# Small steps of each norm in a fixed sequence, weights split on one engine, and the values' product ahead of the gates'

## The chip, the core and the metric

The kernel runs on one core of a Trainium2 chip, as one program. TensorE (PE) multiplies matrices, VectorE (DVE), ScalarE (ACT) and GpSimd (POOL) do the rest, and SyncE (SP) issues the transfers. Each engine works through its own instructions in the order in which they were written; semaphores make it wait for others. The metric is the time of an execution on the device in microseconds (us), less is better.

## The reference

The input is 256 tokens of width 1024 in float32. A first block of two layers (window, stick-breaking and block attention with gates, then a gated feed-forward part with a short convolution) ends in an rms norm. The change touches only what the second block shares with it, the split of weights, and the second block's own layers:

```python
for l in range(2):
    hcat = x @ w_in[l]   # r_q r_k r_v r_g (256 each), c_q c_kv k_r, m_q m_k m_v m_o (256 each), m_i m_f
    ret   = retention(rope(r_q), rope(r_k), r_v)                       # 4 heads of 64
    ret_out   = silu(r_g) * (head_norm(ret) * ret_gn_w[l])
    att_out   = mla_attention(...)                                     # 8 heads of 64, from c_q, c_kv, k_r
    hcell     = num / max(abs(den), exp(-m_t))                         # mlstm(m_q, m_k, m_v, m_i, m_f)
    mlstm_out = head_norm(sigmoid(m_o) * hcell) * mlstm_gn_w[l]
    x = layer_norm(ALPHA * x + concat(ret_out, att_out, mlstm_out) @ w_out[l])
    f = swiglu(x) if l == 0 else moe_swiglu(x)                         # 8 experts of 3584, each token in 2
    x = layer_norm(ALPHA * x + f)

def head_norm(x, w, n):          # per token and head
    mu, var = mean(x), mean((x - mu)**2)
    return (x - mu) * rsqrt(var + 1e-5) * w
```

## The kernel before

Each float32 product is made of three (`mm3`): an operand is split into a high part that PE takes exactly and a low part with the rest, and high·high, high·low and low·high are added up. So every weight is split on the way. SP loads it in pieces of 1 MB into buffers (`raw`, and parts of `b24a`, `b24b`, `const` and `mixed` that are lent later on); ACT copies 128x1024 of it into `whi` (`Weights.high`); then `raw - whi` is written to `wlo` (`Weights.low`). This subtraction is called the split here. There are about a thousand of them, and `low` chooses the engine: POOL, if a layer norm is under way (`g.calm`) or if POOL would be done earlier than DVE by more than the constant `POOL`, and DVE otherwise. `g.quiet` keeps splits off POOL. Splits are made ahead of use into five pairs of buffers (`PIECES`).

The order on each engine is fixed when the program is built. A planner in Python writes the matmuls in sequence, and keeps a model of time for every engine (`Meter`). Between matmuls, `Ctx.tick` looks through lists of tasks (`first`, `urgent`, `tasks`, `heads`) and writes what the model holds to be ready. A task is a Python generator: at each `yield` it gives way to others, or waits for a condition. Because a split belongs to `urgent`, it can come between any two steps of a norm that are parted by a `yield`. All instructions are recorded under one line, L163, in the wrapper `Counted`.

A layer of the second block runs as follows. `second_mixer` multiplies x by parts of `w_in` in the order of `plan_second` and queues the heads (retention `ret_pair`, mLSTM `mlstm_pair`, latent attention `mla`), whose small matmuls come between those of the projections. `ret_norm` and `mlstm_norm` call `head_norm` for each half t of the tokens (128 each), transpose the result on PE (matmuls with `const`) and split it into the operand of the product with `w_out`. That product adds up eight blocks of 128 rows in the order `MIX_ORDER`: blocks 0 and 1 are the retention's, 2 to 5 the attention's, 6 and 7 the mLSTM's. `out_ln` runs this product and `layer_norm` on its result: addition to x with statistics in two halves of 512 columns, the small steps of `rstd` (a scale on POOL, then a power −0.5 on POOL), two steps on x with mean and weight, two with the factor and bias. The result is transposed (matmuls of `const` and `X`), split into `hTh` and `hTl` and meets the next weights. Layer 0 has a dense feed-forward part (`dense_ffn`), layer 1 a routing followed by eight experts. The tail of a mixer is the end of this product, where PE waits for the head norms.

Of the kernel before, what the change touches and what calls it, by code (L numbers as in the profile page):

```python
# [17 lines left out]
P = 128  # L18
# [177 lines left out]
class Weights:  # L196
# [67 lines left out]
    def low(self, i, hi, lo, raw, piece, buf, last):  # L264
        g = self.g
        m = g.m
        n = lo.free_size()
        pool = lambda: max(m.t["gpsimd"], m.floor) + 2.3 * n
        if g.calm and pool() > g.calm[0]:
            yield lambda: not g.calm or pool() <= g.calm[0]  # L270
        dve = max(m.t["vector"], m.floor) + 1.04 * n
        eng = g.nc.gpsimd if g.calm or pool() + POOL < dve and not g.quiet else g.nc.vector
        eng.tensor_tensor(lo, raw, hi, op=ALU.subtract)
        self.done[i] = (hi, lo, piece)
        self.low_done += 1
# [47 lines left out]
class Ctx:  # L323
# [5 lines left out]
    def __init__(self, ctx, tc, a):  # L329
# [9 lines left out]
        self.calm = []  # L339
# [208 lines left out]
POOL, SLACK, EARLY, EARLY_MOE = 1000.0, 0.0, 4000.0, 1500.0  # L548
# [725 lines left out]
def last_norm(g, fT, done, X):  # L1274
# [16 lines left out]
    def post(t, o):  # L1291
# [6 lines left out]
        rstd(g, ss[:, 3:4], ss[:, 2:3], D, 1e-6)  # L1298
# [18 lines left out]
def head_norm(g, r, mult, out):  # L1317
# [10 lines left out]
    yield  # L1328
    rs = sm[:, 12:16]
    rstd(g, rs, mv[:, :, 1], 1.0, 1e-5)  # L1330
    yield
    for h in range(4):
        nc.vector.tensor_scalar(r[:, h, :], r[:, h, :], mv[:, h, 0:1], rs[:, h:h + 1], op0=ALU.subtract, op1=ALU.mult)
    g.give(sm)
    nc.vector.tensor_tensor(out, r.rearrange("p h d -> p (h d)"), mult, op=ALU.mult)


def plan_second(g, l):
# [9 lines left out]
    plan_t(g, w, 1952, 512)  # L1348
    plan_t(g, w, 512, 512)
# [10 lines left out]
MIX_ORDER = [2, 3, 4, 5, 6, 7, 0, 1]  # L1360
# [4 lines left out]
def second_mixer(g, x, l, hT, ready):  # L1365
# [104 lines left out]
    def latents(t, o):  # L1470
# [15 lines left out]
        rstd(g, r, ss, 256, 1e-5)  # L1486
# [147 lines left out]
    def ret_norm(t):  # L1634
        yield got("ret", 2)
        yield got(f"sg{t}")
        yield lambda: g.free["t10"] and g.free["small"]
        r = g.take("t10")
        yield from head_norm(g, heads_out["ret"][1][:, t], sg[:, t, :], r)
# [38 lines left out]
    def mlstm_norm(t):  # L1678
        yield got("mlstm", 2)
        yield got(f"so{t}")  # L1680
        yield lambda: g.free["t10"] and len(g.free["small"]) >= 2
        r = g.take("t10")
        hh = heads_out["mlstm"][1]
# [5 lines left out]
        sv = so[:, t, :].rearrange("p (h d) -> p h d", h=4)  # L1689
# [57 lines left out]
    def mvo(t, o):  # L1747
        nc.vector.tensor_copy(vX[:, t, :, 0:64], o[:, 0:256].rearrange("p (h d) -> p h d", h=4))
        g.act(so[:, t, :], o[:, 256:512], AF.Tanh, scale=0.5)
        g.give(o)  # L1750
        done.mark("mv")
        yield
        nc.gpsimd.tensor_scalar(so[:, t, :], so[:, t, :], 1.0, None, op0=ALU.add)
    for t in range(2):
        g.do(count(f"so{t}", mvo(t, o[t])))
# [4 lines left out]
    def rvg(t, o):  # L1760
        nc.scalar.activation(rv[:, t, :], o[:, 0:256], AF.Copy)
        g.act(sg[:, t, :], o[:, 256:512], AF.Tanh, scale=0.5)
        done.mark("rv")
        yield got("along")
        nc.vector.scalar_tensor_tensor(sg[:, t, :], sg[:, t, :], 1.0, o[:, 256:512], op0=ALU.add, op1=ALU.mult)
        g.give(o)
        yield
        nc.gpsimd.tensor_tensor(sg[:, t, :], sg[:, t, :], rw, op=ALU.mult)
    for t in range(2):
        g.do(count(f"sg{t}", rvg(t, o[t])))  # L1770
# [6 lines left out]
    def over():  # L1777

        yield got("mla", 4)
        g.quiet += 1  # L1780
# [3 lines left out]
        g.quiet -= 1  # L1784
# [33 lines left out]
def layer_norm(g, x, o, wb, bb, free=None, half=None):  # L1818
# [6 lines left out]
    g.calm.append(max(g.m.floor, g.m.t["vector"]) + 2700)  # L1825
# [769 lines left out]
```

## Time and profile before

| | |
|---|---|
| median of 3 runs | 2377.19 us (2376.48 to 2380.56) |
| the profiled execution | 2376.09 us, span 2374.4 us |
| mean granted clock of PE | 0.991 |
| PE, DVE, ACT, POOL busy | 97%, 78%, 63%, 17% of the span |
| POOL, splits of `raw` | 35, 93.5 us in all, 2672 ns each |
| DVE, splits of `raw` | 597, 748.4 us in all, 1280 ns each |

Of 40 slices of the span, the first 23 or so are the first block and the mixers with the dense part; from about 1400 us on the experts run, in which the transfers' share of the 16 engines is 0.9 and above, and from 1640 us on POOL does nothing. The granted clock is 1.00 nearly everywhere; it falls in a few short stretches, around and behind waits of PE. What a wait of PE costs is its own length and what such a stretch adds.

### The profile page before, as it was taken

The page shows a single profiled execution, that of the slowest core. Times are in us where ns is not written, and L with a number is a line of the kernel's source. Part 1 is how long each engine was busy: PE and PEld are TensorE (multiplying, and loading weights), DVE is VectorE, ACT ScalarE, POOL GpSimd, SP SyncE. Part 2 cuts the span into 40 slices and gives each one's busy share as a digit, 9 for nine tenths or more (in the row PEclk, how much of TensorE's full clock was granted, in tenths as well). Part 3 has the DMA queues.
Part 4 walks back from the last instruction along what each step waited for, and adds up shares of the span by engine and source line. Part 5 has one row for each costly group of instructions (what it writes and reads, how often), then busy time and mean ns, then how long its engine had stood idle before and what let it go on. Part 6 is the DMA issues. An engine that isn't in the chain of part 4 may idle for free. (4 is left out here: it accounts for less than half of the span.)

```text
span 2374.4 us, 36554 instructions
## 1 busy us (share of the span) xinstructions
PE 2298.7 (97%) x13593; PEld 1958.9 (83%) x13593; DVE 1851.4 (78%) x2618; ACT 1490.6 (63%) x2144; POOL 407.3 (17%) x417
## 2 busy tenths in 40 slices
PE   8999999999999999989999889989999999999997
PEld 7799999988999988779978668767888767888764
DVE  6666897665589856775568778899888899898898
ACT  4664566465646645634436457777777787777785
POOL 5202343224043312220022320220000000000000
PEclk9999999999999999999999999999999999999999
DMA  7345555543555564355654569999999899999894
GB/s 246 124 127 193 167 187 186 191 136 115 177 178 162 194 215 156 107 169 187 221 156 135 200 246 333 348 378 375 366 344 364 332 389 397 371 337 360 321 373 171
DMA packets 267951, 577.77 MB, mean 243 GB/s; under 512 B 12818, under 2 KB 138354, under 8 KB 267508
## 3 DMA queue, kind: packets, MB, share of 16 engines
q1 hardware_dynamic: 267764, 575.35, 68.4%
q8 instruction: 108, 1.77, 0.3%
q14 instruction: 79, 0.65, 0.1%
HBM read 574.27 MB, written 1.05 MB: 242 GB/s over the span
## 5 line engine op out<-in xcount | busy, mean ns | idle before, releaser
L163 DVE TENSOR_TENSOR wlo<-raw,whi 128x1024 fp32r<-128x1024 f32 (+1 forms) x597 | 748.4, 1280 | 195.1 <-ACT whi L163 191.9
L163 ACT ACTIVATE whi<-raw 128x1024 fp32r<-128x1024 f32 (+1 forms) x632 | 643.0, 1042 | 169.3 <-PE bank L163 140.8
L163 PE MATMUL bank<-hTh,whi 128*128 128x256 f32 x1064 | 306.1, 288 | 0.2 <-ACT const L163 0.2
L163 PE MATMUL bank<-hTl,whi 128*128 128x256 f32 x1064 | 301.4, 283 | 0.0
L163 PE MATMUL bank<-hTh,wlo 128*128 128x256 f32 x1064 | 301.3, 283 | 0.0
L163 PE MATMUL bank<-whi,b8c 128*128 128x512 f32 x752 | 247.7, 398 | 0.0
L163 PE MATMUL bank<-whi,b8a 128*128 128x512 f32 x672 | 234.2, 403 | 0.0
L163 DVE TENSOR_TENSOR wlo<-b24b,whi 128x1024 fp32r<-128x1024 f32 x168 | 201.5, 1244 | 13.5 <-ACT whi L163 12.8
L163 PEld LDWEIGHTS bank<-hTh,whi 128*128 128x128 f32 x1064 | 201.8, 190 | 3.6 <-issue 1.5
L163 PEld LDWEIGHTS bank<-hTh,wlo 128*128 128x128 f32 x1064 | 201.6, 190 | 0.1
L163 PEld LDWEIGHTS bank<-hTl,whi 128*128 128x128 f32 x1064 | 201.7, 190 | 0.0
L163 PE MATMUL bank<-whi,hTl 128*128 128x512 f32 (+2 forms) x540 | 196.5, 386 | 0.0
L163 PE MATMUL bank<-wlo,b8a 128*128 128x512 f32 x448 | 182.0, 406 | 8.9 <-DVE wlo L163 5.4
L163 ACT ACTIVATE whi<-b24b 128x1024 fp32r<-128x1024 f32 x172 | 174.0, 1056 | 13.9 <-PE bank L163 12.7
L163 POOL TENSOR_TENSOR wlo<-raw,whi 128x1024 fp32r<-128x1024 f32 (+1 forms) x35 | 93.5, 2672 | 515.0 <-ACT whi L163 492.3
L163 PE MATMUL bank<-wlo,b8c 128*128 128x512 f32 x432 | 173.5, 402 | 6.1 <-DVE wlo L163 6.1
L163 PEld LDWEIGHTS bank<-whi,b8c 128*128 128x128 f32 x752 | 140.9, 188 | 31.7 <-issue 1.0
L163 PEld LDWEIGHTS bank<-whi,b8a 128*128 128x128 f32 x672 | 126.3, 189 | 30.3 <-issue 2.4
L163 DVE TENSOR_TENSOR wlo<-b24a,whi 128x1024 fp32r<-128x1024 f32 x121 | 143.2, 1224 | 5.8 <-ACT whi L163 5.6
L163 PE MATMUL bank<-whi,hTh 128*128 128x512 f32 (+2 forms) x348 | 138.3, 397 | 0.0
L163 POOL TENSOR_SCALAR small<-small 128x1 f32<-128x1 f32 (+2 forms) x15 | 4.4, 293 | 779.5 <-DVE small L163 778.6
L163 PE MATMUL bank<-b8a,whi 128*128 128x256 f32 x480 | 136.3, 284 | 0.0
(317 smaller groups left out, 5229.4 us busy)
## 6 DMA issues: line engine op xcount, KB each, us to landing
raw<-in_w_in_dram SPq DMA_DIRECT2D x68, 1024.0 KB
raw<-in_moe_w_up_dram SPq DMA_DIRECT2D x47, 1024.0 KB
raw<-in_w_up_dram SPq DMA_DIRECT2D x44, 1024.0 KB
raw<-in_moe_w_gate_dram SPq DMA_DIRECT2D x43, 1024.0 KB
raw<-in_moe_w_down_dram SPq DMA_DIRECT2D x34, 1024.0 KB
b24b<-in_moe_w_up_dram SPq DMA_DIRECT2D x33, 1024.0 KB
b24b<-in_moe_w_down_dram SPq DMA_DIRECT2D x32, 1024.0 KB
b24a<-in_moe_w_down_dram SPq DMA_DIRECT2D x27, 1024.0 KB
```

Of the source, the lines that this page charges most:

```text
L163: r = f(*a, **kw)
```

## The change

Splits are made by DVE alone and not while `g.quiet` is set, which `layer_norm` now sets from its small steps to its last step on x. The small steps are written without a `yield` between them, the first of them on DVE. In `out_ln` the norm of the second half of the tokens waits until that of the first is written. In `head_norm` the scaling by mean and factor moves from DVE to ACT (Identity with scale and bias), for which a shift −mean·rs is made; the multiplication by the gate or weight is done by the callers. `mlstm_norm` divides by the denominators with one broadcast multiplication per half. In `plan_second` and `second_mixer` the product for the values (r_v, m_v) comes ahead of that for the gates (r_g, m_o). `MIX_ORDER` puts the retention's blocks ahead of the mLSTM's.

```diff
 class Weights: def low(self, i, hi, lo, raw, piece, buf, last):
-        pool = lambda: max(m.t["gpsimd"], m.floor) + 2.3 * n
-        if g.calm and pool() > g.calm[0]:
-            yield lambda: not g.calm or pool() <= g.calm[0]
-        dve = max(m.t["vector"], m.floor) + 1.04 * n
-        eng = g.nc.gpsimd if g.calm or pool() + POOL < dve and not g.quiet else g.nc.vector
-        eng.tensor_tensor(lo, raw, hi, op=ALU.subtract)
+        if g.quiet:
+            yield lambda: not g.quiet
+        g.nc.vector.tensor_tensor(lo, raw, hi, op=ALU.subtract)
...
-def rstd(g, out, var, n, eps):
+def rstd(g, out, var, n, eps, by="vector"):
-    g.nc.gpsimd.tensor_scalar(out, var, 1.0 / n, eps, op0=ALU.mult, op1=ALU.add)
+    getattr(g.nc, by).tensor_scalar(out, var, 1.0 / n, eps, op0=ALU.mult, op1=ALU.add)
     g.nc.gpsimd.tensor_tensor(out, out, g.half[:, :m], op=ALU.pow)
...
 def head_norm:
-    yield
-    rs = sm[:, 12:16]
+    rs, shift = sm[:, 12:16], sm[:, 16:20]
     rstd(g, rs, mv[:, :, 1], 1.0, 1e-5)
+    nc.vector.tensor_scalar(shift, mv[:, :, 0], -1.0, None, op0=ALU.mult)
+    nc.gpsimd.tensor_tensor(shift, shift, rs, op=ALU.mult)
     yield
     for h in range(4):
-        nc.vector.tensor_scalar(r[:, h, :], r[:, h, :], mv[:, h, 0:1], rs[:, h:h + 1], op0=ALU.subtract, op1=ALU.mult)
+        nc.scalar.activation(out[:, h, :], r[:, h, :], AF.Identity, scale=rs[:, h:h + 1], bias=shift[:, h:h + 1])
     g.give(sm)
-    nc.vector.tensor_tensor(out, r.rearrange("p h d -> p (h d)"), mult, op=ALU.mult)
+    yield
...
 def plan_second:
-    plan_t(g, w, 1952, 512)
-    plan_t(g, w, 512, 512)
+    for c in (0, 256):
+        for k0 in (0, 4):
+            k = slice(k0 * P, (k0 + 4) * P)
+            g.w.add([w[k, 512 + c:768 + c], w[k, 1952 + c:2208 + c]], 4, 512, [(0, 2, 0, 512), (2, 4, 0, 512)])
...
-MIX_ORDER = [2, 3, 4, 5, 6, 7, 0, 1]
+MIX_ORDER = [2, 3, 4, 5, 0, 1, 6, 7]
...
 def ret_norm:
-        yield from head_norm(g, heads_out["ret"][1][:, t], sg[:, t, :], r)
+        yield from head_norm(g, heads_out["ret"][1][:, t], r.rearrange("p (h d) -> p h d", h=4))
+        nc.gpsimd.tensor_tensor(r, r, rw, op=ALU.mult)
+        yield got(f"sg{t}")
+        nc.vector.tensor_tensor(r, r, sg[:, t, :], op=ALU.mult)
...
 def mlstm_norm:
-        for h in range(4):
-            nc.vector.scalar_tensor_tensor(hh[:, t, h, :], hh[:, t, h, :], den[:, h:h + 1], sv[:, h, :],
-                                           op0=ALU.mult, op1=ALU.mult)
+        nc.vector.tensor_tensor(hh, hh, den[:, :, None].to_broadcast([P, 4, 64]), op=ALU.mult)
-        yield from head_norm(g, hh[:, t], mw, r)
+        yield got(f"so{t}")
+        nc.vector.scalar_tensor_tensor(hh, so[:, t, :].rearrange("p (h d) -> p h d", h=4), 1.0, hh, op0=ALU.add,
+                                       op1=ALU.mult)
+        yield from head_norm(g, hh, r.rearrange("p (h d) -> p h d", h=4))
+        nc.vector.tensor_tensor(r, r, mw, op=ALU.mult)
...
 def layer_norm:
-    g.calm.append(max(g.m.floor, g.m.t["vector"]) + 2700)
...
-    yield
     rstd(g, r, mv[:, 1:2], 1.0, 1e-5)
-    del g.calm[0]
+    g.quiet += 1
...
+    g.quiet -= 1
...
 def out_ln: def post(t, o):
-        yield from layer_norm(g, x[t], o, wb[:, 0], wb[:, 1], lambda: g.give(*o), half)
+        if t:
+            yield done.got("norm")
+        yield from done.count("norm", layer_norm(g, x[t], o, wb[:, 0], wb[:, 1], lambda: g.give(*o), half))
```

The three places of which the prediction speaks, in the order in which the instructions are written. In these rows `t_…` are tiles of 256 columns, `small` and `mixed` here hold the norms' small values.

DVE in the mixer's tail of layer 0, before: two head norms end with four scalings (TENSOR_SCALAR, 128x64) and a multiplication each, with splits between them.

```order
L163 TENSOR_SCALAR t_0_65<-t_0_65,small_83 128x64 x4
L163 TENSOR_TENSOR t_1_69<-t_0_65,b24a_8801 128x256
L163 TENSOR_TENSOR wlo_100<-raw_62,whi_99 128x1024
L163 TENSOR_TENSOR wlo_102<-raw_63,whi_101 128x1024
L163 TENSOR_SCALAR t_2_67<-t_2_67,small_82 128x64 x4
L163 TENSOR_TENSOR t_3_71<-t_2_67,b8c_8426 128x256
L163 TENSOR_TENSOR wlo_94<-raw_63,whi_93 128x1024
L163 TENSOR_SCALAR t_2_67<-t_2_67,mixed 128x64 x4
L163 TENSOR_TENSOR t_0_68<-t_2_67,b8c_8426 128x256
```

The same place now, from the mLSTM's second half on: statistics, two small steps, two splits, and the last multiplications of both halves.

```order
L163 SCALAR_TENSOR_TENSOR t_2_67<-b24a_8801,t_2_67 128x256
L163 BN_STATS hst_9759<-t_2_67 128x6 x4
L163 BN_AGGR mixed<-hst_9759 128x2 x4
L163 TENSOR_SCALAR mixed<-mixed 128x4 x2
L163 TENSOR_TENSOR wlo_102<-raw_63,whi_101 128x1024
L163 TENSOR_TENSOR wlo_94<-raw_63,whi_93 128x1024
L163 TENSOR_TENSOR t_0_68<-t_0_68,b8c_8426 128x256
L163 TENSOR_TENSOR t_1_69<-t_1_69,b8c_8426 128x256
```

The scalings have left DVE, and no head norm but the mLSTM's stands at the end.

PE in the same tail, before: the eight transposes (`const`) of all four head norms stand together.

```order
L163 MATMUL bank_87<-whi_95,b24b_8802 128x512 x2
L163 MATMUL bank_87<-wlo_96,b24b_8802 128x512
L163 MATMUL bank_88<-const,t_4_72 128x128 x2
L163 MATMUL bank_85<-const,t_1_69 128x128 x2
L163 MATMUL bank_86<-const,t_3_71 128x128 x2
L163 MATMUL bank_91<-const,t_0_68 128x128 x2
L163 MATMUL bank_89<-whi_97,b24b_8802 128x512 x2
```

Now the retention's (`t_3_71`, `t_4_72`) come early, right behind the first matmuls after the mLSTM's output (`b_41_8991,mixed`), and the mLSTM's (`t_0_68`, `t_1_69`) 30 matmuls on:

```order
L163 MATMUL bank_87<-b_41_8991,mixed 128x128 x3
L163 MATMUL bank_90<-whi_101,b24b_8802 128x512 x2
L163 MATMUL bank_90<-wlo_102,b24b_8802 128x512
L163 MATMUL bank_91<-whi_101,b24b_8802 128x512 x2
L163 MATMUL bank_91<-wlo_102,b24b_8802 128x512
L163 MATMUL bank_85<-const,t_3_71 128x128 x2
L163 MATMUL bank_86<-whi_93,b24b_8802 128x512 x2
L163 MATMUL bank_86<-wlo_94,b24b_8802 128x512
L163 MATMUL bank_89<-const,t_4_72 128x128 x2
```

Four of the eight transposes have moved ahead, four stay at the end.

DVE in the second half's layer norm behind the mixer of layer 0, before (`X` is the norm's tile; POOL makes three further splits in this stretch):

```order
L163 SCALAR_TENSOR_TENSOR X<-X,bank_90 128x512
L163 BN_STATS bns_9885<-X 128x6
L163 BN_AGGR mixed<-bns_9885 128x2
L163 SCALAR_TENSOR_TENSOR X<-X,mixed,b8c_8426 128x512 x2
L163 TENSOR_TENSOR wlo_100<-raw_62,whi_99 128x1024
L163 TENSOR_TENSOR wlo_94<-raw_63,whi_93 128x1024
L163 SCALAR_TENSOR_TENSOR X<-X,mixed,b8c_8426 128x512 x2
L163 TENSOR_TENSOR hTl_9829<-bank_89,hTh_9828 128x4x128
```

The same place now:

```order
L163 SCALAR_TENSOR_TENSOR X<-X,bank_91 128x512
L163 BN_STATS bns_9887<-X 128x6
L163 BN_AGGR mixed<-bns_9887 128x2
L163 TENSOR_SCALAR mixed<-mixed 128x1
L163 SCALAR_TENSOR_TENSOR X<-X,mixed,b8c_8426 128x512 x4
L163 TENSOR_TENSOR wlo_98<-raw_61,whi_97 128x1024
L163 TENSOR_TENSOR wlo_100<-raw_62,whi_99 128x1024
L163 TENSOR_TENSOR wlo_102<-raw_62,whi_101 128x1024
L163 TENSOR_TENSOR wlo_94<-raw_63,whi_93 128x1024
L163 TENSOR_TENSOR hTl_9835<-bank_87,hTh_9834 128x4x128
```

The four steps on `X` stand together, and four splits behind them.

## Rows read from the trace of the kernel before

**Rows 1.** The page: busy time, share and instructions of each engine.

```profile
PE 2298.7 (97%) x13593; PEld 1958.9 (83%) x13593; DVE 1851.4 (78%) x2618; ACT 1490.6 (63%) x2144; POOL 407.3 (17%) x417
```

**Rows 2.** Waits of PE, whole span: us in total, times, longest.

```profile
PE bank L163 <- DVE wlo L163: 16.6, 27, 2.1
PE bank L163 <- DVE t L163: 14.1, 6, 3.3
PE bank L163 <- DMA mixed<-in_norm_mix_dram: 4.9, 1, 4.9
```

**Rows 3.** Waits of PE from 1000 to 1031 us, the tail in layer 0.

```profile
PE bank L163 <- DVE t L163: 6.0, 3, 3.2
```

**Rows 4.** Waits of PE from 1330 to 1357 us, the tail in layer 1.

```profile
PE bank L163 <- DVE t L163: 5.1, 2, 3.3
PE bank L163 <- ACT b24b L163: 0.9, 1, 0.9
```

**Rows 5.** Windows: us; PE, PEld, DVE, ACT, POOL busy; PE's clock, DMA share, GB/s.

```profile
1013.00:1022.00 9.00, 7.17 (x21) 5.40 (x20) 5.67 (x12) 2.66 (x4) 0.00 (x0) 0.55 0.94 323
1342.00:1349.00 7.00, 6.68 (x24) 5.29 (x25) 3.96 (x7) 2.27 (x3) 0.00 (x0) 0.76 0.91 315
1511.00:1630.00 119.00, 109.33 (x466) 79.55 (x464) 109.47 (x103) 93.37 (x112) 24.00 (x7) 0.97 0.97 369
1879.00:1993.00 114.00, 109.16 (x466) 77.13 (x465) 108.55 (x110) 93.79 (x111) 0.00 (x0) 1.00 0.99 386
```

**Rows 6.** Timeline of DVE, tail of layer 0: start, duration, operation.

```profile
1001.96 0.59 DVE L163 BATCH_NORM_STATS2 hst<-t 128x6 f32<-128x64 f32 x4
...
1008.39 0.43 DVE L163 TENSOR_TENSOR t<-t,b24a 128x256 f32<-128x256 f32 x1
1008.73 2.35 DVE L163 TENSOR_TENSOR wlo<-raw,whi 128x1024 fp32r<-128x1024 f32 x2
```

**Rows 7.** Timeline of POOL in the same tail.

```profile
1002.99 0.19 POOL L163 TENSOR_SCALAR small<-small 128x4 f32<-128x4 f32 x1
...
1005.09 1.07 POOL L163 TENSOR_SCALAR mixed<-mixed 128x4 f32<-128x4 f32 x1 [0.81 <-DVE mixed L163]
```

**Rows 8.** Timeline of all engines in the routing.

```profile
1381.54 0.22 DVE L163 TENSOR_TENSOR t<-small 128x64 f32<-128x64 f32 x1
...
1382.00 4.70 POOL L163 TENSOR_TENSOR wlo<-b24a,whi 128x1024 fp32r<-128x1024 f32 x2 [14.74 <-ACT whi L163]
1382.06 2.42 DVE L163 TENSOR_TENSOR t<-small,b24a 128x64 f32<-128x64 f32 x1
...
1384.52 2.27 DVE L163 TENSOR_TENSOR t<-t,b24a 128x64 f32<-128x64 f32 x1
```

**Rows 9.** Waits of PE from 1376 to 1412 us, routing and the first expert's start.

```profile
PE bank L163 <- DVE t L163: 3.0, 1, 3.0
PE bank L163 <- DVE wlo L163: 1.7, 1, 1.7
```

**Rows 10.** Waits of PE from 1195 to 1262 us, the norm behind the dense part.

```profile
PE bank L163 <- DVE X L163: 3.0, 2, 1.8
PE bank L163 <- POOL b8b L163: 0.6, 1, 0.6
```

**Rows 11.** Waits of PE from 1031 to 1046 us, the norm behind layer 0's mixer.

```profile
PE bank L163 <- DVE hTl L163: 1.0, 2, 0.7
PE bank L163 <- DVE X L163: 0.8, 2, 0.5
```

**Rows 12.** Tile `wlo` from 1640 us on: minimum, median, maximum in ns.

```profile
L163 DVE TENSOR_TENSOR wlo<-raw,whi x187: 681/1216/1228, 1639.5 to 2354.6; 128x1024 fp32r<-128x1024 f32 x183, 128x512 fp32r<-128x512 f32 x4
```

**Rows 13.** Timeline of DVE in the norm behind the dense part.

```profile
1216.43 4.88 DVE L163 SCALAR_TENSOR_TENSOR X<-X,small,b8c 128x512 f32<-128x512 f32 x2
...
1222.70 1.41 DVE L163 SCALAR_TENSOR_TENSOR X<-X,small,b8c 128x512 f32<-128x512 f32 x2 [0.43 <-POOL small L163]
```

**Rows 14.** Timeline of DVE at the first expert's start.

```profile
1404.82 4.55 DVE L163 TENSOR_TENSOR wlo<-const,whi 128x1024 fp32r<-128x1024 f32 x2
```

More of the change, by code (lines that the diff above doesn't have):

```diff
@@ L338, in __init__ @@
         self.quiet = 0
-        self.calm = []
         self.early = EARLY
@@ L547 @@
 T10, SMALL, PIECES = 6, 10, 5
-POOL, SLACK, EARLY, EARLY_MOE = 1000.0, 0.0, 4000.0, 1500.0
+SLACK, EARLY, EARLY_MOE = 0.0, 4000.0, 1500.0
 TABLES = {"natural_log_exp_and_others": (AF.Exp, AF.Ln), "exp_and_others": (AF.Exp, AF.Tanh),
@@ L1297, in post @@
         nc.gpsimd.tensor_tensor(ss[:, 2:3], ss[:, 0:1], ss[:, 1:2], op=ALU.add)
-        rstd(g, ss[:, 3:4], ss[:, 2:3], D, 1e-6)
+        rstd(g, ss[:, 3:4], ss[:, 2:3], D, 1e-6, "gpsimd")
         yield
@@ L1313, with head_norm @@
 MOST, GAP = 2, 6000.0
-def head_norm(g, r, mult, out):
+def head_norm(g, r, out):
     nc = g.nc
@@ L1485, in latents @@
         yield
-        rstd(g, r, ss, 256, 1e-5)
+        rstd(g, r, ss, 256, 1e-5, "gpsimd")
         yield
@@ L1635, in ret_norm @@
         yield got("ret", 2)
-        yield got(f"sg{t}")
+        yield got("along")
         yield lambda: g.free["t10"] and g.free["small"]
         r = g.take("t10")
-        yield from head_norm(g, heads_out["ret"][1][:, t], sg[:, t, :], r)
+        yield from head_norm(g, heads_out["ret"][1][:, t], r.rearrange("p (h d) -> p h d", h=4))
+        nc.gpsimd.tensor_tensor(r, r, rw, op=ALU.mult)
+        yield got(f"sg{t}")
+        nc.vector.tensor_tensor(r, r, sg[:, t, :], op=ALU.mult)
         yield "bank"
@@ L1679, in mlstm_norm @@
         yield got("mlstm", 2)
-        yield got(f"so{t}")
         yield lambda: g.free["t10"] and len(g.free["small"]) >= 2
         r = g.take("t10")
-        hh = heads_out["mlstm"][1]
+        hh = heads_out["mlstm"][1][:, t]
         sm = g.take("small")
@@ L1745, in second_mixer, with values, gates_out @@
     o = gemm_t(g, hT, 512)
-    def mvo(t, o):
-        nc.vector.tensor_copy(vX[:, t, :, 0:64], o[:, 0:256].rearrange("p (h d) -> p h d", h=4))
+    def values(t, o):
+        nc.vector.tensor_copy(vX[:, t, :, 0:64], o[:, 256:512].rearrange("p (h d) -> p h d", h=4))
+        done.mark("mv")
+        nc.scalar.activation(rv[:, t, :], o[:, 0:256], AF.Copy)
+        done.mark("rv")
+        g.give(o)
+    for t in range(2):
+        g.do(lambda t=t, o=o: values(t, o[t]))
+    o = gemm_t(g, hT, 512)
+    def gates_out(t, o):
+        g.act(sg[:, t, :], o[:, 0:256], AF.Tanh, scale=0.5)
         g.act(so[:, t, :], o[:, 256:512], AF.Tanh, scale=0.5)
+        done.mark(f"so{t}")
+        yield
+        nc.vector.scalar_tensor_tensor(sg[:, t, :], sg[:, t, :], 1.0, o[:, 0:256], op0=ALU.add, op1=ALU.mult)
         g.give(o)
-        done.mark("mv")
-        yield
-        nc.gpsimd.tensor_scalar(so[:, t, :], so[:, t, :], 1.0, None, op0=ALU.add)
     for t in range(2):
-        g.do(count(f"so{t}", mvo(t, o[t])))
-    o = gemm_t(g, hT, 512)
[L1760 to L1770, printed above, removed]
+        g.do(count(f"sg{t}", gates_out(t, o[t])))
     def ready_k(k, t):
@@ L1779, in over @@
         yield got("mla", 4)
-        g.quiet += 1
         for t in range(2):
@@ L1783, in over @@
             yield got(f"rnorm{t}")
-        g.quiet -= 1
         g.give(*keep, *[b for b, _ in heads_out.values()])
@@ L1834, in layer_norm @@
         free()
-    yield
     rstd(g, r, mv[:, 1:2], 1.0, 1e-5)
-    del g.calm[0]
+    g.quiet += 1
     for n in range(2):
```

2 lines of the change are left out of this document (removed).

## The prediction, made before the change was run

> **What bounds the kernel now.** I read the busy shares first: TensorE (PE) is busy 2298.7 of 2374.4 us [rows 1], so only its idle time and the stretches in which it runs slowly can be won, 75.7 us of idle time in all. The list of what PE waited for comes next: VectorE (DVE), by splits of weights (16.6) and by the mixer's output `t` (14.1); a transfer ended only one long wait (4.9, at the start) [rows 2]. Then each stage by itself. In the two mixer tails PE waits 6.0 and 5.1 + 0.9 us for the head norms [rows 3, 4], and is granted about half its clock right behind: 0.55 over 9 us, 0.76 over 7 us [rows 5]. Around the two norms at the end of a mixer PE loses 1.8 us [rows 11], at the one behind the dense FFN 3.6 [rows 10], in the routing 3.0 and 1.7 [rows 9]. In the MoE the second expert takes 119 us, the fifth 114, with 466 matmuls and 109.3 and 109.2 us of PE work; POOL is busy 24.0 us in the one (seven splits) and not at all in the other [rows 5].
>
> **The key row** is in the routing. A DVE step on 64 columns takes 0.22 us; while POOL makes two splits (4.70 us), two such steps take 2.42 and 2.27 [rows 8]. In a layer norm two steps on 512 columns take 4.88 beside POOL splits and 1.41 without [rows 13]. From 1640 us on POOL makes no split, and 187 DVE splits lie between 681 (half width) and 1228 ns, median 1216 [rows 12]. So a POOL split of 2.35 us costs DVE about what it lasts (2.42 − 0.22 = 2.2 and 2.27 − 0.22 = 2.05), where the same split on DVE costs 1.22. POOL's help is worth nothing to DVE, and in a chain for which PE waits it is worth less than nothing.
>
> **1. All splits on DVE.** Price of one: 1.22 [rows 12], gain where one stood beside DVE work: about 2.1 [rows 8].
> - Routing: the two slow steps give back 2.2 + 2.05, one split comes into the same chain, +1.22: 3.0 us, just PE's wait there [rows 9]. −3.0.
> - First expert's start: PE's 1.7 for `wlo` [rows 9] comes of a pair of DVE splits that takes 4.55 [rows 14] instead of 2.4, one of them beside a POOL split. Three in a row on DVE take 3.7, less than the pair now. −1.7.
> - Second expert: order and operands become those of the fifth, so 114 instead of 119 [rows 5]. −5.0. DVE's busy time there stays near 109 us of 114.
> - First block (16 of the 45 POOL splits): no wait of PE in it names a split, so 0. Cover: PE's own queue of matmuls; if it is gone, 16 × 1.22 = 19.5 is the most it could cost, which I think remote, as DVE gives back what POOL's splits took.
>
> **2. Mixer tails.** Removed from DVE: sixteen scalings per layer (now ACT's, four Identity steps per norm). ACT's four are in no row; between 0.59 (DVE's four statistics of 64 columns [rows 6]) and 1.7 (four steps at the 0.43 of 256 columns), I take 1.0. The retention's output now comes early, and only the mLSTM's is last, behind 36 instead of 33 matmuls. From the last correction of the mLSTM's weights DVE has: five splits at 1.18 (half of 2.35), 5.9; ten steps on 256 columns, 0.35 each from start to start (1008.39 to 1008.73), 3.5; two norms' statistics, 1.2, and their small steps, about as much, an estimate; two denominators of three small steps, about 1.1, an estimate [rows 6]: 12.9. PE has the 12 matmuls of the mLSTM's output (about 1.5 with its start), 36 matmuls at 0.234 (109.16 us over 466 in the fifth expert [rows 5]) and four transposes, 10.3 in all. PE so waits 2.6, plus what POOL and ACT hang over the two splits (pow, which I take at the 1.07 of the longest small step [rows 7], Identity 1.0, a small multiply 0.2, and 0.9 for three hand-overs, an estimate; less two splits, 2.4): 0.8. 3.4 in one piece, where before there were three pieces. A 3.2-us wait was followed by the slow clock in both tails, so I keep half a stretch of it: 1.8. Sum after: 5.2. Before: 6.0 + 7.17 × 0.45 = 9.2 in layer 0, 6.0 + 6.68 × 0.24 = 7.6 (and 0.3 just ahead) in layer 1 [rows 3 to 5]. −4.0 and −2.7. Bounds: nothing gained (0) and all gone (−9.2 and −7.9).
>
> **3. Layer norms.** Behind the mixers: X comes early enough, so its 0.8 [rows 11] goes; the hTl wait (0.7) stays. But splits are held from the small steps to the last step on X: the order of DVE shows `wlo_98` behind four X steps, where PE needs it in front of the second transposes. From hTl on DVE has the addition and statistics (1.4), aggregate and small step (0.4), four X steps (2.8 [rows 13]) and the split (1.2): 5.8; PE has 18 matmuls, 4.2. It waits 1.6. Together 2.3 against 1.8 in layer 0, with the rounding +0.6 each, +1.2. Behind the FFN: X's first wait (1.8 of 3.0) goes, since two steps fall from 4.88 to 1.41. Two splits (2.2) that POOL had now stand between t=1's additions, which eats that 1.8, and `b8b` is held behind X: it is ready about when POOL had it, and PE is there 1.8 earlier: 0.6 + 1.8 − 0.3 = 2.1 instead of 3.6 [rows 10]. −1.5. Behind the held splits queue the hTl steps of the second half, and PE needs them only some 30 matmuls (7 us) on.
>
> **4. What costs nothing.** The values' product first: PE's order is the same outside the norms and tails, and values were not waited for. The first small step on DVE (0.17 beside POOL's 0.19 to 1.07 [rows 7]) is within the terms above. Eight loads of 1 MB are now cut into runs of half the length: no row prices that; between 0 and one wait as long as the 4.9 that a transfer once cost [rows 2]; I take 0, as PE waits for no transfer in the mixers and SP's queue is hundreds of matmuls ahead.
>
> **Sum:** −3.0 − 1.7 − 5.0 − 4.0 − 2.7 + 1.2 − 1.5 = −16.7 us. The profiled execution took 2376.1, 1.1 under the median of the runs (2377.2). 2377.2 − 16.7 = 2360.5.
>
> **Rivals.**
> - *Tails as long as before.* POOL's small steps stay in the chain, and now meet a DVE that splits without pause. A small POOL step took 1.07 beside a DVE split where its like took 0.19 [rows 7]: 0.9 lost per step. With pow, the shift's multiply and the retention's 256-column multiply in each tail that is 3 to 4 us per tail, which takes the 6.7 back: 2367. For it: the row; against: the retention's part has 6 us to spare. The Trainium skill states this as a rule that cuts against the change (SBUF — State Buffer, section "Who interferes with whom"): a DVE instruction with two SBUF inputs and a GpSimd instruction that reads SBUF use one shared pair of ports, and who starts first holds it to the end. By that rule the trace's long rows come out on both engines, as rows 7 and 8 show.
> - *Held splits burst.* After each of eight norms up to four splits (4.7) come at once; if each pair of norms costs one more wait of 1.2 with the slow clock behind half of them, +5: 2365.5. Against: PE's order has 30 matmuls there.
> - *Transfers take the MoE's gain.* DMA share is 0.97 in the second expert and 0.99 in the fifth [rows 5]; if weights now arrive later than DVE wants them, the 6.7 of the MoE stay: 2367. Against: in the fifth the same share goes with 114.
> - *Tails vanish:* wait and slow clock go, 17.1 instead of 6.7: 2350. Against: two splits stand ahead of the last step.
> - *DVE becomes the bound (slower).* If the long rows were not POOL's doing, DVE takes seven more splits in the second expert, where it is busy 109.5 of 119 [rows 5]: +8.5; and ten in the norms' chains: +12.2; with the tails' −6.7 that is +14, 2391. It decides once a DVE split beside nothing is no shorter than now. The Trainium skill bears on it (Perfetto Trace Analysis, section "Optimizing Scalar/DVE Operations"): a saturated DVE is a reason to hand work to GPSIMD, with the reserve that a shared port may make it useless. Rows 8 and 12 speak for the reserve.
>
> **How the numbers follow.** Forecast 0.42; tails unchanged 0.20; burst 0.10; transfers 0.10; tails vanish 0.10; slower 0.06; no effect 0.02. The first five are each faster by over 0.2% (4.8 us, about the least that a measurement tells from none), but two or three of the bad ones together reach 2372 to 2375: I move 0.07 from there to "same" and 0.01 to "slower". Faster 0.84, same 0.09, slower 0.07. The range takes in the vanishing tails, and two of the bad cases at once (2360.5 + 6.7 + 5): 2350 to 2372.
>
> **What would show it.** No split on POOL, and no DVE step of 64 columns over 0.3 us in the routing; the second expert as long as the fifth; in each tail one wait of 3 to 4 us on `t`, with less than 7 us at half clock; a new wait of 1 to 2 us for `wlo` in front of the second transposes of X. It is wrong if DVE's splits stay long without POOL's, if PE starts to wait for splits in the first block, or if PE waits for transfers in the MoE.

## The result, and the profile after

The changed kernel takes 2345.05 us (median of 4 runs, 2344.63 to 2346.34); the kernel before, run beside it, 2376.84 (4 runs, 2374.57 to 2380.56). The ratio is 0.9868, interval [0.9853, 0.9884]: 31.8 us less. The prediction had the sign and about half the size: 2360.5, and its range ended at 2350. The profiled execution took 2344.63 us, with a span of 2342.9 and a granted clock of 0.996 instead of 0.991.

The page of the changed kernel, busy time per engine, against [rows 1]:

```profile
PE 2287.4 (98%) x13593; PEld 1952.3 (83%) x13593; DVE 1838.7 (78%) x2647; ACT 1501.4 (64%) x2176; POOL 282.2 (12%) x360
```

DVE has taken over 45 splits and a number of small steps, and is busy 12.7 us less all the same. POOL lost 125.1 us of work, 93.5 of it the splits of `raw`. Waits of PE in the changed kernel over the whole span, against [rows 2]:

```profile
PE bank L163 <- DVE wlo L163: 13.6, 30, 1.5
PE bank L163 <- DMA mixed<-in_norm_mix_dram: 4.6, 1, 4.6
PE bank L163 <- DVE t L163: 4.4, 4, 1.2
PE bank L163 <- DVE b8b L163: 2.8, 2, 2.6
```

The waits for `t` fall from 14.1 to 4.4. Those for `wlo` only from 16.6 to 13.6, but the longest is 1.5 instead of 2.1.

**Where the time went.** PE has 13593 matmuls in both kernels, so the n-th of one can be laid beside the n-th of the other. The table gives how much a stage became shorter (start of the same matmul after, less before, differences between the stage's ends), at places where the order is the same on both sides. The profile of before is one execution; a second one was taken later (experiment 8), and the two columns show what belongs to an execution and not to the kernel. The last two columns are the profiles of the first two experiments, against the profile before. The last one is of an execution of 2379.26 us, 4.2 above the median of its kernel's runs, so its sum (+2.7) is not what that kernel is worth (−2.6, below).

| stage, us of the trace before | predicted | after, against the profile before | after, against its second execution | splits alone | all but the splits |
|---|---|---|---|---|---|
| first block, to 960 | 0 | −4.5 | 0.0 | −3.6 | −0.2 |
| mixer of layer 0, to 1034 | −4.0 | −5.7 | −4.4 | −1.0 | −3.7 |
| norm behind it, to 1195 | +0.6 | −0.4 | −0.4 | +0.2 | +3.0 |
| norm behind the dense part, to 1254 | −1.5 | −1.8 | −3.3 | −2.5 | +1.0 |
| mixer of layer 1 and its norm, to 1376 | −2.1 | −6.6 | −6.5 | +0.3 | +0.5 |
| routing, first expert's start, to 1511 | −4.7 | −5.0 | −7.8 | −5.0 | +1.5 |
| second expert, to 1660 | −5.0 | −8.1 | −9.5 | −8.1 | +0.5 |
| rest | 0 | −0.1 | 0.0 | −0.1 | 0.0 |
| sum | −16.7 | −32.0 | −31.9 | −19.7 | +2.7 |

Windows of the changed kernel, with the columns of [rows 5]: the tail of layer 0, the tail of layer 1, and the second expert (the same 466 matmuls):

```profile
1007.00:1016.00 9.00, 7.49 (x27) 5.93 (x28) 5.08 (x8) 5.04 (x9) 0.00 (x0) 0.81 0.83 261
1326.00:1335.00 9.00, 7.20 (x32) 5.80 (x33) 6.61 (x11) 5.04 (x9) 0.25 (x1) 1.00 0.85 272
1487.18:1598.50 111.32, 108.73 (x466) 77.08 (x464) 108.70 (x111) 95.08 (x113) 0.00 (x0) 1.00 1.01 397
```

The second expert takes 111.3 us instead of 119, at full clock; the slow clock is gone from the tail of layer 1 and halved in that of layer 0. Timeline of DVE in the changed kernel's tail of layer 0 (start, duration, operation), from the last correction of the mLSTM's weights on, against [rows 6]:

```profile
991.76 1.02 DVE L163 SCALAR_TENSOR_TENSOR mixed<-bank,mixed 128x384 f32<-128x384 f32 x2
...
1004.40 0.24 DVE L163 TENSOR_SCALAR mixed<-mixed 128x4 f32<-128x4 f32 x2
1004.55 2.35 DVE L163 TENSOR_TENSOR wlo<-raw,whi 128x1024 fp32r<-128x1024 f32 x2
1006.83 0.41 DVE L163 TENSOR_TENSOR t<-t,b8c 128x256 f32<-128x256 f32 x1
1008.47 0.42 DVE L163 TENSOR_TENSOR t<-t,b8c 128x256 f32<-128x256 f32 x1 [1.23 <-ACT t L163]
```

POOL there, against [rows 7]:

```profile
1002.80 1.01 POOL L163 TENSOR_TENSOR small<-small,half 128x4 f32<-128x4 f32 x1 [6.29 <-DVE small L163]
1003.89 0.20 POOL L163 TENSOR_TENSOR small<-small 128x4 f32<-128x4 f32 x1
1004.65 1.98 POOL L163 TENSOR_TENSOR mixed<-mixed,half 128x4 f32<-128x4 f32 x1 [0.57 <-DVE mixed L163]
```

ACT, the four Identity steps of the last norm:

```profile
1007.00 1.43 ACT L163 ACTIVATE t<-t,mixed 128x64 f32<-128x64 f32 x4 [1.44 <-POOL mixed L163]
```

and PE, the mLSTM's output and the two waits that are left:

```profile
994.65 2.84 PE L163 MATMUL bank<-b,mixed 128*128 128x128 f32 x24
...
1007.29 0.44 PE L163 MATMUL bank<-const,t 128*128 128x128 f32 x2 [0.99 <-DVE t L163]
1008.95 0.52 PE L163 MATMUL bank<-const,t 128*128 128x128 f32 x2 [1.21 <-DVE t L163]
```

PE waits 2.2 us in two pieces, where it waited 6.0. The chain is the one that was forecast: statistics, small steps, power on POOL, four steps on ACT, last multiplication. The power that runs into two splits takes 1.98 us, the one half before it 1.01.

### The profile page after: what moved, and what is told of

Read it like the earlier page. It is cut to its first block, busy times and chain, and to the rows that moved or that the text cites. A ratio compares the mean times of both kernels' runs of the same rounds, so it can differ in the third digit from the quotient of the medians.

```text
span 2342.9 us, 36545 instructions
## 1 busy us (share of the span) xinstructions
PE 2287.4 (98%) x13593; PEld 1952.3 (83%) x13593; DVE 1838.7 (78%) x2647; ACT 1501.4 (64%) x2176; POOL 282.2 (12%) x360
## 5 line engine op out<-in xcount | busy, mean ns | idle before, releaser
L163 DVE TENSOR_TENSOR wlo<-raw,whi 128x1024 fp32r<-128x1024 f32 (+1 forms) x632 | 776.3, 1256 | 197.3 <-ACT whi L163 192.0
L163 POOL TENSOR_TENSOR small<-small,half 128x1 f32<-128x1 f32 (+2 forms) x15 | 13.3, 884 | 1201.1 <-DVE small L163 1200.7
L163 PE MATMUL bank<-wlo,hTh 128*128 128x512 f32 (+2 forms) x348 | 133.3, 383 | 2.9 <-DVE wlo L163 2.9
L163 ACT ACTIVATE whi<-b24a 128x1024 fp32r<-128x1024 f32 x124 | 126.3, 1057 | 14.2 <-PE bank L163 13.8
```

Of the source, the lines that this page charges most:

```text
L163: r = f(*a, **kw)
```

## The experiments

**1 and 2. The splits alone, and all but the splits.** The first is the kernel before with this edit:

```diff
-        eng = g.nc.gpsimd if g.calm or pool() + POOL < dve and not g.quiet else g.nc.vector
-        eng.tensor_tensor(lo, raw, hi, op=ALU.subtract)
+        g.nc.vector.tensor_tensor(lo, raw, hi, op=ALU.subtract)
```

The second is the changed kernel with the old choice of engine, and `calm` in place of the hold:

```diff
-        g.nc.vector.tensor_tensor(lo, raw, hi, op=ALU.subtract)
+        eng = g.nc.gpsimd if g.calm or pool() + POOL < dve and not g.quiet else g.nc.vector
+        eng.tensor_tensor(lo, raw, hi, op=ALU.subtract)
...
-    g.quiet += 1
+    del g.calm[0]
```

> The kernel before, with all splits on VectorE and nothing else changed (none held). Theory A: every gain outside the mixer tails comes of the splits alone, so the stages give what they gave in the full change: start and first block -4.4, norm behind the dense part -1.8, routing -3.2, first expert's start -1.9, second expert -7.7, tails 0, sum -19: about 2358. Rival B: only the stages that I had priced follow the splits (routing -3.0, first expert -1.7, second expert -5.0), and the rest comes of the new sequences: about 2367. Rival C: without the new sequences VectorE's longer queue costs in the norms' chains what it gives elsewhere: 2370 or more.

> The changed kernel with the old choice of engine for the splits (GpSimd takes some again, in norms and when it would be done first; no hold in the layer norm). Theory A: it keeps the tails' 12 and loses the 19 of the splits: about 2364. Rival B: the tails need the splits off GpSimd too, and lose half their gain: about 2370. Rival C: the new sequences alone are worth most of it: 2355 or less.

Measured: splits alone 2356.49 (ratio 0.9913 [0.9897, 0.9930]), −21.2; all but the splits 2375.06 (0.9989 [0.9980, 0.9999]), −2.6. The first is what theory A gave (2358). The second lies outside all three theories: A gave 2364, B 2370, C 2355 or less, and all of them credited the new sequences with gains that do not come without the splits. Together the two give 23.8, and the whole change 31.8: 8.0 us come only from both. By the three intervals that difference is known to about 6 us, an estimate, so it is there, but its size is rough. By the table most of it lies in the norms behind the mixers and in the mixer of layer 1 (−6.6 with both, +0.3 and +0.5 with one). What the splits on POOL do to the new sequences is seen in the second kernel's norm behind layer 0's mixer, DVE:

```profile
1022.52 3.58 DVE L163 SCALAR_TENSOR_TENSOR X<-X,mixed,b8c 128x512 f32<-128x512 f32 x2
1026.53 1.42 DVE L163 SCALAR_TENSOR_TENSOR X<-X,mixed,b8c 128x512 f32<-128x512 f32 x2 [0.44 <-POOL mixed L163]
...
1033.46 5.66 DVE L163 TENSOR_TENSOR wlo<-raw,whi 128x1024 fp32r<-128x1024 f32 x3
```

and POOL:

```profile
1023.14 2.40 POOL L163 TENSOR_TENSOR wlo<-raw,whi 128x1024 fp32r<-128x1024 f32 x1 [10.25 <-ACT whi L163]
...
1033.26 2.51 POOL L163 TENSOR_TENSOR wlo<-raw,whi 128x1024 fp32r<-128x1024 f32 x1
```

The two steps on X that meet the POOL split take 3.58 instead of 1.42, three DVE splits 5.66 instead of about 3.5. What the shorter chain gains in that tail (−3.7) is nearly lost again in the norm behind it (+3.0), where POOL's splits stretch the steps. Splits on DVE, for their part, win little in the tail (−1.0) while the old chain is its end: there the first kernel still waits 5.4.

```profile
PE bank L163 <- DVE t L163: 5.4, 2, 3.3
```

**3. The scaling back on DVE.**

```diff
-        nc.scalar.activation(out[:, h, :], r[:, h, :], AF.Identity, scale=rs[:, h:h + 1], bias=shift[:, h:h + 1])
+        nc.vector.tensor_scalar(out[:, h, :], r[:, h, :], mv[:, h, 0:1], rs[:, h:h + 1], op0=ALU.subtract, op1=ALU.mult)
```

> The changed kernel with the head norm's scaling back on VectorE (four TENSOR_SCALAR per norm, no shift). Theory A: VectorE's work sets the tail; 16 steps of 0.24 us more per layer stand in its row, so each tail's wait grows from 2.2 us to about 4 with a longer slow clock behind: +2 to +3.7 per tail, 2349 to 2352. Rival B: ScalarE's four steps take 1.43 us and GpSimd's multiply 0.25 where VectorE's take 0.98, and the last norm waits for them (1.23 us in the trace), so the move back costs nothing: 2344 to 2346.

Measured 2348.88 (0.9883 [0.9867, 0.9900]), +3.8 (here and below the median less the changed kernel's 2345.05): one wait of 2.9 us per tail instead of 2.2 in two, and the slow clock in layer 1. That is nearer to theory A than to B, but the wait grew by 0.7 where A had almost 2. Moving the scaling to ACT is worth about 2 us a layer (1.0 in layer 0 and 2.9 in layer 1 by the profile).

**4. No hold of splits in the layer norms.**

```diff
 def layer_norm:
-    g.quiet += 1
...
-    g.quiet -= 1
```

> The changed kernel without the hold of splits in the layer norms. Theory A: the hold only turns a wait for X into a wait for a split (1.46 us in each norm behind a mixer, 2.6 behind the dense part), so nothing changes beyond 2 us: 2343 to 2347. Rival B: the hold costs its new waits, 5.6 us in all: about 2340. Rival C: without it X comes later by two splits in each of eight norms, with slow clock behind some: 2350 or more.

Measured 2346.42 (0.9874 [0.9857, 0.9890]), +1.4, as theory A had it and not more than its runs spread: the waits for `wlo` (1.5) and `b8b` (2.6) go, others and some slow clock come. The hold is worth about nothing.

**5 and 6. The old order of the mixed product, and the gates' product first** (in the second, the two blocks of `second_mixer` are exchanged together with their weights).

```diff
-MIX_ORDER = [2, 3, 4, 5, 0, 1, 6, 7]
+MIX_ORDER = [2, 3, 4, 5, 6, 7, 0, 1]
```

```diff
-    for c in (0, 256):
+    for c in (256, 0):
```

> The changed kernel with the old order of blocks in the product with w_out (2 to 5, then 6 and 7, then 0 and 1). Theory A: the mLSTM's blocks come 12 matmuls (2.8 us) sooner for the first half of the tokens, so each tail's wait of 2.2 us grows to about 5, with one more stretch of slow clock (1.7): +2.8 to +4.5 per tail, 2351 to 2354. Rival B: the planner writes all transposes of the head norms where the last is ready, whatever the order, so nothing moves: 2344 to 2347.

> The changed kernel with the gates' product ahead of the values' (weights loaded in that order too). Theory A: retention and mLSTM can start only behind the second product, so their last matmuls move towards the tail and its wait grows by 2 to 4 us per layer: 2349 to 2353. Rival B: the heads wait for the conv and the gates' small steps anyway, so the order of the two products is worth nothing: 2344 to 2347.

Measured 2353.42 (0.9904 [0.9887, 0.9920]), +8.4, and 2355.09 (0.9911 [0.9894, 0.9927]), +10.0. Waits of PE in the tail of layer 0, from 1000 us on, in the first of the two:

```profile
PE bank L163 <- DVE t L163: 4.9, 2, 3.8
```

and in the second:

```profile
PE bank L163 <- DVE t L163: 4.2, 2, 3.2
PE bank L163 <- DVE b24b L163: 1.3, 1, 1.3
```

The first is as theory A had it, the second 2 us above it. Either order costs more than the two tails together were expected to give (6.7). With the gates first the chain ends later in both layers, and in layer 1 by more than theory A allowed (5.7 us by the profile, against 4). This is not the way back to the kernel before, though: there, one product made m_v with m_o and the next r_v with r_g, so neither all values nor all gates came first. What the new division into values and gates is worth against that old one, no run shows. The prediction gave it no gain ("what costs nothing").

**7. Idle work on POOL.** The changed kernel, and in the fifth expert seven subtractions on POOL (in two halves of 512 columns each) whose result nobody reads:

```diff
+        if i - self.moe >= 4 * 84 and i - self.moe < 5 * 84 and (i - self.moe) % 12 == 6:
...
+            for h in range(2):
+                c = slice(512 * h, 512 * h + 512)
+                g.tc.nc.gpsimd.tensor_tensor(g.scrap, g.still[:, c], piece[0][:, c], op=ALU.subtract)
```

> The changed kernel with seven extra subtractions on GpSimd in the fifth expert, each on 128x1024 in two halves, beside the splits of VectorE; nobody reads their result, and no instruction of the other engines moves. Theory A (the two engines shut each other out): each costs VectorE about what it lasts, 2.1 us, 15 in all; VectorE is busy 108 of the expert's 114 us, so the expert grows by 9 to 15 us: 2354 to 2360. Rival B (the long rows of VectorE had another cause): the expert stays at 114 and the time at 2344 to 2347.

Measured 2362.77 (0.9943 [0.9926, 0.9959]), +17.7, of which 16.3 in that expert. Its window there (the extra time is in it):

```profile
1847.00:1978.00 131.00, 114.38 (x469) 77.89 (x469) 120.75 (x112) 95.35 (x113) 32.15 (x14) 0.99 0.93 342
```

and the changed kernel's:

```profile
1847.00:1961.00 114.00, 109.16 (x466) 77.14 (x465) 108.58 (x110) 93.79 (x111) 0.00 (x0) 1.00 0.99 385
```

DVE, with the same splits, is busy 12.2 us longer. PE's waits for `wlo` in the expert grow from 4.7 to 13.5. One meeting of the two, DVE and then POOL, in that kernel:

```profile
1855.82 3.89 DVE L163 TENSOR_TENSOR wlo<-raw,whi 128x1024 fp32r<-128x1024 f32 x2
```

```profile
1854.98 3.65 POOL L276 TENSOR_TENSOR t<-X,whi 128x512 f32<-128x512 f32 x2 [510.70 <-ACT whi L163]
```

Two splits take 3.89 instead of 2.35. This is the key row of the prediction, shown by itself. But not all of the 16.3 is of this kind, which is why it passes the 15 of theory A. The fourth subtraction took far longer on POOL than the other six (3.50 to 4.25):

```profile
1909.31 10.28 POOL L276 TENSOR_TENSOR t<-X,whi 128x512 f32<-128x512 f32 x2 [12.18 <-ACT whi L163]
```

It reads a buffer of `whi`, so ACT could not write the next high part into it, and PE waited for ACT. Waits of ACT and of PE in the window of that kernel:

```profile
ACT whi L163 <- POOL t L276: 7.0, 2, 6.3
PE bank L163 <- ACT whi L163: 2.6, 1, 2.6
```

Around this one PE loses 5.4 us, part of it at a slow clock (0.91 from 1910 to 1930 us); why it took so long is open. Around the other six PE loses 1.5 to 2.2 us each, 10.9 in all. So work that nobody waits for, on an engine that had nothing to do, costs PE about 1.8 us per subtraction, and more if it also keeps a buffer.

**8. The kernel before once more**, unchanged, for a second profile.

> The kernel before once more, for a second trace. In the profile of before the two stages of the first block around 280 to 380 and 725 to 850 us took 2.3 us more than in the changed kernel, without a wait of PE, at 119.9 ns a matmul instead of 118.4. Theory A: that belongs to the kernel (GpSimd's splits): the second trace shows it again. Rival B: it differs from execution to execution: 118.4 ns in the second trace.

Measured 2376.04, as the first. But in it the slow clock lies elsewhere (in the routing, for one: 0.62 from 1381 to 1390, where the first profile has 1.00), and its first block is 4.4 us shorter than in the first profile; 3.0 of that are in the first 100 us, where PE's waits, mostly for transfers, are 1.8 shorter. So the first block's −4.5 is the executions' own, but for some 0.5 us each between 270 and 370 and between 725 and 840 us, which both pairs hold (1.1 and 1.2 in the first pair); in the second execution PE waits there for a `wlo`, 0.3 us each time. That is half of what was asked, between the two theories.

**9 and 10. Splits held in the mLSTM's head norm too, and that without the hold in the layer norms** (the tenth takes the lines of experiment 4 out as well), to win the last 2.2 us.

```diff
 def mlstm_norm:
+        g.quiet += 1
         yield from head_norm(g, hh, r.rearrange("p (h d) -> p h d", h=4))
         nc.vector.tensor_tensor(r, r, mw, op=ALU.mult)
+        g.quiet -= 1
```

> The changed kernel, and splits of weights are also held in the mLSTM's head norm, from its statistics to its last multiplication. In DVE's order the last multiplications of both halves now stand ahead of the two splits that lay in front of them. Theory A (what is left of the tail's wait is the two splits and the power on POOL that they stretch from 1.01 to 1.98 us): of each tail's 0.99 + 1.21 about 1.4 is left, less if the power falls back to 1.0, and the slow clock behind layer 0's goes: 0.8 to 2.5 us per tail, 2340 to 2344. Rival B: the first of the two splits is now late for the products that stand right behind the transposes, and PE waits for wlo what it no longer waits for t: 2345 to 2348.

> The kernel before this one (splits held in the mLSTM's head norm), without the hold in the layer norms. Theory A (each hold is priced by what it keeps waiting, and the holds do not touch each other): the waits for wlo behind the mixers (1.5 each) and for b8b behind the dense part (2.6) go and the X steps come later by the splits between them, as in the run without the hold, which was level within 1.4 us: one run's length within 2 us of the other, 2339 to 2345. Rival B: splits freed in the layer norms fill DVE ahead of the norm of the second half, and the result is 3 us or more longer.

Measured 2351.99 (0.9895 [0.9878, 0.9911]) and 2348.82 (0.9888 [0.9870, 0.9906]): both longer than the changed kernel, by 6.9 and 3.8. DVE in the first one's tail of layer 0:

```profile
1007.59 0.42 DVE L163 TENSOR_TENSOR t<-t,b8c 128x256 f32<-128x256 f32 x1 [0.95 <-ACT t L163]
1009.57 0.43 DVE L163 TENSOR_TENSOR t<-t,b8c 128x256 f32<-128x256 f32 x1 [1.56 <-ACT t L163]
1009.91 2.35 DVE L163 TENSOR_TENSOR wlo<-raw,whi 128x1024 fp32r<-128x1024 f32 x2
1012.18 0.74 DVE L163 TENSOR_TENSOR b24b<-bank,b24b 128x256 fp32r<-128x256 f32 x2
```

Its PE, from 1000 us on:

```profile
PE bank L163 <- DVE b24b L163: 1.9, 1, 1.9
PE bank L163 <- DVE t L163: 1.5, 1, 1.5
```

For the ninth this is rival B's kind of loss, at another place than it named and larger than its 2345 to 2348: the held splits are written right behind the last multiplication, ahead of the low part of the transposed result (`b24b`), and PE waits for that. The two splits in the tail had been filling time in which DVE waits for POOL and ACT (0.95 and 1.56 us of idle time here). On the tenth run both theories failed: it is 3.2 us shorter than the ninth, where A allowed 2 either way and B wanted it 3 longer.

**11 and 12. The halves' norms not in sequence, and the first small step on POOL.**

```diff
-        if t:
-            yield done.got("norm")
```

```diff
-def rstd(g, out, var, n, eps, by="vector"):
+def rstd(g, out, var, n, eps, by="gpsimd"):
```

> The changed kernel without the one line by which the layer norm of the second half of the tokens waits for that of the first. Theory A (the sequence matters only through the order of the X steps behind the mixers and the dense part; with every split on DVE there is little to come between): only the four norms change, by 0 to +1.5 us each, 2344 to 2349. Rival B (the sequence is what lets the splits' gain come through, the 8.0 us that splits alone and the rest alone leave over): 2350 to 2353.

> The changed kernel with the first small step of each norm back on POOL (scale and shift by eps), everything else as changed. Theory A: one more hand-over between DVE and POOL and a POOL step of 0.2 to 1.1 us stands in each norm's chain, and PE waits for it only in the two tails and at the norm behind the dense part: 0.5 to 1.5 us each, 2346 to 2350. Rival B: DVE's other steps (the shift) cover it, and nothing changes: 2344 to 2346.

Measured 2353.62 (0.9905 [0.9889, 0.9922]), +8.6: rival B's size (2350 to 2353), a little above it. It is lost behind the mixers (2.8 us in layer 0 and, with the slow clock, 4.4 in layer 1). PE in the tail and norm of layer 0, in place of the changed kernel's 0.3 (`X`), 0.7 (`hTl`) and 1.5 (`wlo`):

```profile
PE bank L163 <- DVE hTl L163: 2.2, 1, 2.2
PE bank L163 <- DVE t L163: 2.2, 2, 1.2
PE bank L163 <- DVE X L163: 1.7, 1, 1.7
```

and 2349.46 (0.9887 [0.9871, 0.9904]), +4.4, as theory A had it: in the tail 2.8 for `t` and 1.9 for `wlo` instead of 2.2 and 1.5, behind the dense part 3.3 for `b8b` instead of 2.6 with a slow clock behind it. A POOL step that lasts 0.19 there makes each of these waits 0.4 to 0.7 longer: it costs more by its hand-over than by itself. None of the kernels tried beats the changed one.

## Why the prediction was wrong, and where it was right

The direction and the key row came out as forecast; the sum did not. It was 15.5 us short (2360.5 against 2345.05), and the time lies below the range. No term had the wrong sign but the small one of the norms; the step that failed is the size of two terms, and both are too small against either execution of the kernel before: the mixer of layer 1 with its norm (−2.1, measured −6.6 and −6.5) and the second expert (−5.0, measured −8.1 and −9.5). Every other stage is within 1.0 of its forecast in at least one of the two columns.

- **The key row: right.** Routing and the first expert's start, −4.7, came as −5.0, all of it with the splits alone. (Against the second execution it is −7.8, of which 2.8 is that execution's slow clock there.) There the steps on 64 columns of [rows 8] take 0.22 to 0.23. The seventh run shows the price from the other side, 1.8 for the 2.1 of the prediction. The Trainium skill has a rule (SBUF — State Buffer, section "Who interferes with whom") that the two engines share a pair of ports, locked by whoever starts first. The trace agrees: rows come out long on DVE (2.42 for 0.22) and on POOL (1.98 for 1.01). The Trainium skill (Perfetto Trace Analysis, section "Optimizing Scalar/DVE Operations") advises to hand work to GPSIMD when DVE is full, with the reserve that for these two engines it might not help. This kernel confirms the reserve: taking the splits off POOL gave 21.2 us.
- **The second expert: a failed step.** "Order and operands become those of the fifth, so 114" took a neighbour's time for this stage's own sum. Before the change, the waits of PE in this stage are

```profile
PE bank L163 <- DVE wlo L163: 6.1, 5, 2.1
PE bank L163 <- POOL wlo L163: 3.4, 2, 3.3
```

 after it (1487 to 1599 us)

```profile
PE bank L163 <- DVE wlo L163: 2.5, 8, 0.6
```

 and in the fifth expert, of which the 114 was taken,

```profile
PE bank L163 <- DVE wlo L163: 4.7, 10, 1.4
```

 So 7.0 us of waits go, and not the 4.8 that stand between 9.5 and 4.7. That is nearly all of the 7.7 measured to 1630 us. Before the change there were also two stretches at about half clock inside the stage:

```profile
1526.00:1530.00 4.00, 3.96 (x8) 2.14 (x8) 2.92 (x3) 0.60 (x1) 0.00 (x0) 0.57 1.00 361
1584.00:1588.00 4.00, 4.00 (x8) 1.96 (x8) 1.21 (x2) 2.56 (x4) 0.00 (x0) 0.57 1.05 387
```

 By themselves they are worth 2 × 4.0 × 0.43 = 3.4. But PE's busy time over the whole stage fell only from 109.33 to 108.73, so just 0.6 of that is left in the sum. Why the second expert waits less than the fifth, no run shows; with the splits alone it takes 111.4 us too.
- **The tails: mechanism right, the wait and the clock behind it mis-sized.** The chain that sets the end is the one in the prediction, but both of its sides were counted short. Counted from the last correction of the mLSTM's weights (DVE, until 992.8), the chain takes 16.2 us instead of 13.7, and PE's own way to the last transposes 14.0 instead of 10.3; the wait is the difference, 2.2 instead of 3.4. On PE's side the mLSTM's output was counted as 12 matmuls, "about 1.5"; it has 24 and takes 2.84. PE also starts it only 1.9 us behind that correction, with matmuls of the product with `w_out` in between. On the chain's side the four Identity steps take 1.43 instead of 1.0, the power 1.98 instead of 1.07, and DVE idles 1.8 us for POOL and ACT. That errors of 2.5 and 3.7 us leave a wait only 1.2 off is luck. "Half a stretch" of slow clock, 1.8, was kept for both tails; that of layer 0 kept 7.49 × 0.19 = 1.4, that of layer 1 none. So layer 1 loses 2.2 of the 7.9 before, where 5.2 was forecast: this is the larger part of its miss. Layer 0 loses 3.6 of the 9.2 before, near the table's −5.7; against the second execution, in which the old tail had less slow clock (0.73 from 1009 to 1018 us), it is −4.4. In both layers some 0.7 us go ahead of the tail, for which there was no term.
- **Norms behind the mixers: the new wait as forecast, the net not.** A wait of 1.6 for `wlo` was to come; 1.5 came, in both layers. The second waits for X and `hTl` (0.55 and 0.23 in layer 0) went, which leaves +0.7 in waits, about as forecast. Yet the stage gained 0.4. The other 1.0 is time around the stops that is in no wait: the eight transposes of X, for one, take 0.79 us up to the next product, where they took 1.35. That a sequence of the two halves is needed at all was not seen: without it 1.7 and 2.2 are waited for X and `hTl`.
- **Behind the dense part: right**, −1.8 for −1.5 (−3.3 against the second execution); the wait for `b8b` is 2.6, forecast 2.1, and both waits for X (3.0) went, not only the first.
- **The first block: 0, and about −1 belongs to the change.** "No wait of PE in it names a split" misread the profile, which has one of 0.3 for `wlo` in the first 100 us; the second execution has two of 0.3 and the changed kernel none. Most of the −4.5 is the profiled execution's own.
- **The rivals.** Those that took gains back (tails as before, burst, transfers, DVE the bound) did not come true in the time; transfers took none, with a DMA share of 1.01 in the second expert. The row on which "tails as before" rested did: a POOL step that meets DVE's splits takes 1.0 us longer (1.98 for 1.01), but only one such step in each tail. "Tails vanish" was nearest in time (2350) and not in kind, as both waits are still there.
- **Two parts together.** The prediction priced each stage with all edits at once and had no term for either part alone, so the 8.0 us that come only from both do not explain the miss. They say that the gain cannot be divided among the edits by adding up their shares.

## What to carry to other kernels

Price a stage by its own waits, read in its own window, and not by a neighbour that looks alike; and count the instructions on both sides of a wait from the order before a duration is put to them. Work put on an engine that shares a resource with the busiest one is not free because the engine idles: unread subtractions on POOL cost PE 1.8 us each here. Where two edits shorten the same chain, one by its steps and one by what stretches them, both together can give more than the sum, as here.

## What the runs showed of the hardware

Which steps of DVE a split on POOL stretches can be seen in the kernel before, in the norm behind layer 1's mixer. DVE:

```profile
1360.29 0.68 DVE L163 SCALAR_TENSOR_TENSOR X<-X,bank 128x512 f32<-128x512 f32 x1
1361.01 0.69 DVE L163 BATCH_NORM_STATS2 bns<-X 128x6 f32<-128x512 f32 x1
1361.73 0.21 DVE L163 BATCH_NORM_AGGREGATE small<-bns 128x2 f32<-128x12 f32 x1
1361.98 1.88 DVE L163 SCALAR_TENSOR_TENSOR X<-X,small,b8c 128x512 f32<-128x512 f32 x2
```

POOL:

```profile
1360.23 2.42 POOL L163 TENSOR_TENSOR wlo<-raw,whi 128x1024 fp32r<-128x1024 f32 x1 [3.82 <-ACT whi L163]
```

While POOL's split runs, the addition that reads `bank` (PSUM) and the statistics with one input keep their 0.68 and 0.69 us; the pair on X with mean and weight, all in SBUF, takes 1.88 instead of 1.41. Two operands in SBUF are not the only case, though. In the first block a TENSOR_SCALAR on four columns, with one tensor to read, takes 2.12 us where its like takes 0.17, and ends with POOL's split. DVE, then POOL:

```profile
153.55 2.12 DVE L163 TENSOR_SCALAR mixed<-mixed 128x4 f32<-128x4 f32 x1
```

```profile
153.27 2.38 POOL L163 TENSOR_TENSOR wlo<-raw,whi 128x1024 fp32r<-128x1024 f32 x1 [19.51 <-ACT whi L163]
```

When the clock falls stays open. Two waits of 0.99 and 1.21 us were followed by a slow stretch in layer 0 (0.81 over 9 us) and two as long by full clock in layer 1 of the same execution; in the twelfth run waits of 1.6 and 1.2 were followed by full clock in both tails. Two executions of the kernel before have the slow clock in different stages (up to 2.8 us of difference in one stage) and agree in the sum within 0.1 us.
